# Values and transposed probabilities of a 32-row branch laid out in 128-row tiles, with zero rows below

## The chip, the cores and the metric

The kernel runs on one core of a Trainium2 chip. The metric is the device time of one execution in microseconds (us); the time before is the median of three runs. Engines are named as the profile names them: PE (TensorE, matrix products), PEld (its weight loads), DVE (VectorE), ACT (ScalarE), POOL (GpSimd), SP (SyncE, which issues the DMA transfers).

## The reference

One transformer layer on 512 tokens of width 1024, in float32: a gated feed-forward part (FFN), a mixer of two attention groups, a second FFN, a last norm. The change lies in the first attention group, which adds up three branches per token; the first of them attends to 31 compressed blocks of keys and values:

```python
def nsa_group(q, kc_raw, vc_raw, ...):
    kc = compress_blocks(kc_raw, ...)      # 31 blocks of 32 tokens, stride 16
    vc = compress_blocks(vc_raw, ...)
    ...
    s = jnp.where(mask_c, s - slopes * dist_c, NEG_INF)
    p_cmp = jnp.where(mask_c, jax.nn.softmax(s, axis=-1), 0.0)
    o_cmp = jnp.einsum('bgrtc,bcgd->btgrd', p_cmp, vc)      # contracts over the 31 blocks
    ...
    return g[..., 0:1] * o_cmp + g[..., 1:2] * o_slc + g[..., 2:3] * o_win
```

There are 8 query heads in 2 groups of 4, and the head width is 64.

## The kernel before

The kernel is one long Python program over a scheduling layer: it writes the work down in some order, and the layer fixes a list of instructions for each engine from its own estimate of costs, and the semaphore waits between them. Each engine works through its list in order. Products are made in a 32-bit format that keeps fewer bits (`F32R`), so a value is kept as two parts, high and low: ACT makes the high part by a cast, DVE the low part by a subtraction, and PE makes two or three products in place of one.

The mixer is cut into attention stages. A stage `Nsa(g, i, br)` handles group `g`, query block `i` of 128 tokens and branch `br`. `scores` makes the scores of four heads on PE (lines 838, 839, 918, 922, 923), DVE finds maxima (L911), ACT takes exponentials (L912), DVE and ACT scale them (L973 to L989). `outputs` then goes through a list `work` of blocks of keys. For each one `transposed` lets PE transpose the probabilities of four heads into one bank (L847), ACT copies the high part out (L849) and DVE the low part (L850) into a tile `u`; then `times_values` multiplies both by the values, in two products of 512 columns that add up in the bank `pv` (L884, L885). For the windows of the sequence a block has 128 keys. The compressed branch has one block of 32 rows (31 blocks and one row of zeros): its values are `CV`, a tile of 32 partitions with the two parts of both groups, its probabilities fill `u[:32]`, and its two products contract over 32 rows. It comes last in the list of the stage that closes a query block; with two groups and four query blocks that makes 8 stages and 16 such products. After the last product of a stage `put_o` takes the result out of `pv` (L855, L860, L866, L867); there is one `pv` bank.

While attention runs, pieces of other work (projections, products with the output weights, L207 to L209) are put between its steps on PE; their weights come through `split_next`, which splits a loaded tile into two parts (L97 on ACT, L98 on DVE). Units of 1024 numbers per partition come from one pool, `flat` and `unit`, with 32 buffers (`NU`); each buffer is given out again when the last reader of its tile is done.

```python
NU, NT8, NTMP, NRAW = 32, 4, 10, 4
work.append((cl, slice(0, 32), 32, CV[:, g].rearrange("p a d -> p (a d)")))
```

Of the kernel before, what the change touches and what calls it, by code (L numbers as in the profile page):

```python
# [10 lines left out]
F32R = mybir.dt.float32r  # L11
BF16 = mybir.dt.bfloat16
AF = mybir.ActivationFunctionType
ALU = mybir.AluOpType
AX = mybir.AxisListType

P = 128
# [5 lines left out]
HD = 64  # L23
# [21 lines left out]
def tile_hybrid(ctx, tc, xT, f1_wi, f1_wo, wm_t, wm_n, cw1, cw2, small, wm_oa, wm_ob, wm_oc, f2_wi, f2_wo, const, out):  # L45
    nc = tc.nc
    V, A, PE = nc.vector, nc.scalar, nc.tensor

    sb = ctx.enter_context(tc.tile_pool(name="sb", bufs=1))
    psp = ctx.enter_context(tc.tile_pool(name="psp", bufs=1, space=bass.MemoryType.PSUM))  # L50

    def f(ap):
        return ap.bitcast(F32)

    def ps(tag="mm"):
        return psp.tile([P, 512], F32, tag=tag, name=tag, bufs=NB[tag])
# [8 lines left out]
    def flat(dt=F32R):  # L65
        return sb.tile([P, 1024], dt, tag="u", name="u", bufs=NU)

    def unit(dt=F32R):
        return flat(dt).rearrange("p (a t) -> p a t", a=2)
# [4 lines left out]
    def tmp():  # L74
        return sb.tile([P, 512], F32, tag="tmp", name="tmp", bufs=NTMP)
# [6 lines left out]
    ones = sb.tile([P, P], F32, tag="ones", name="ones")  # L82
# [578 lines left out]
        yield from mm3_steps(o, wh, wl, ALLK, xs, True, True)  # L661


    CV = sb.tile([32, 2, 2, HD], F32R, tag="cv", name="cv")

    def compressed(kv):
        o = ps()
# [55 lines left out]
    def network_o(kv):  # L723
        hT, w2 = state["hT", kv]
        po = ps()
        if kv == 0:
            for c in range(2):
                PE.matmul(po[:HD, :62], w2[:, c, :], hT[:, c, :], start=c == 0, stop=c == 1)
            kc = tmp()
            V.memset(kc[:HD, :64], 0.0)  # L730
            V.tensor_copy(
                kc[:HD, :64].rearrange("p (g c) -> p g c", g=2)[:, :, :NCMP],
                po[:HD, :62].rearrange("p (g c) -> p g c", g=2),
            )
            for g in range(2):
                put_key(kc[:HD, g * 32 : g * 32 + 32], 0, KT[g][0][:, 512:544], KT[g][1][:, 512:544])
        else:
            vc = tmp()
            V.memset(vc[:32, :128], 0.0)
            for g in range(2):  # L740
                for c in range(2):
                    PE.matmul(
                        po[:NCMP, g * HD : (g + 1) * HD], hT[:, c, g * NCMP : (g + 1) * NCMP], w2[:, c, :],
                        start=c == 0, stop=c == 1,
                    )
            V.tensor_copy(vc[:NCMP, :128], po[:NCMP, :128])
            vcv = vc[:32, :128].rearrange("p (g d) -> p g d", g=2)
            A.copy(CV[:, :, 0, :], vcv)
            V.tensor_tensor(CV[:, :, 1, :], vcv, f(CV[:, :, 0, :]), op=ALU.subtract)
        yield 0.6  # L750


# [4 lines left out]
    def put_key(src, g, k1, k2):  # L757

        own = slice(g * HD, (g + 1) * HD)
        oth = slice((1 - g) * HD, (2 - g) * HD)  # L760
        A.copy(k1[own], src)
        V.tensor_tensor(k2[own], src, f(k1[own]), op=ALU.subtract)
        nc.sync.dma_start(f(k1[oth]), f(k1[own]))
        nc.sync.dma_start(f(k2[oth]), f(k2[own]))
# [79 lines left out]
    def transposed(pl, rows, cols):  # L844
        pt = ps()
        for r in range(4):
            PE.transpose(pt[:rows, r * P : (r + 1) * P], pl[r][:, cols], ident)  # L847
        u = unit()
        A.copy(u[:rows, 0, :], pt[:rows, :])  # L849
        V.tensor_tensor(u[:rows, 1, :], pt[:rows, :], f(u[:rows, 0, :]), op=ALU.subtract)  # L850
        return u
# [17 lines left out]
    def times_values(work, pv, first, last):  # L869

        ahead = None
        for n in range(len(work) + 1):
            if n < len(work):
                pl, cols, rows, v = work[n]
                cur = transposed(pl, rows, cols), rows, v
                if n == 0:
                    yield 0.44
            else:
                cur = None
            if ahead is not None:  # L880
                u, rows, v = ahead
                a = first and n == 1
                b = last and n == len(work)
                PE.matmul(pv, v, u[:rows, 0, :], start=a, stop=False)  # L884
                PE.matmul(pv, v, u[:rows, 1, :], start=False, stop=b)  # L885
                yield 0.87 if n < len(work) else 0.43
            ahead = cur

    class Nsa:
# [102 lines left out]
        def outputs(self):  # L992
            g, i, br = self.g, self.i, self.br
            if br != 2:
                state["pv"] = ps("pv")
            pv = state["pv"]

            def values_of(b, kb):
                return VT[b][:, kb, g].rearrange("p a d -> p (a d)")

            if br == 0:
                work = [(self.p, slice(b * P, (b + 1) * P), P, values_of(b, 0)) for b in range(2)]
            else:
                work = [(self.p, slice(kb * P, (kb + 1) * P), P, values_of(br - 1, kb)) for kb in range(i + 1)]
            if br != 1:
                cl = [self.c[:, r, :] for r in range(4)]
                work.append((cl, slice(0, 32), 32, CV[:, g].rearrange("p a d -> p (a d)")))
            yield from times_values(work, pv, br != 2, br != 1)
            if br != 1:
                put_o(pv, g * 2, i)  # L1010

    class Swa:
# [45 lines left out]
        def outputs(self):  # L1058
            g, i, W, c0 = self.g, self.i, self.W, self.c0
            pv = ps("pv")  # L1060
            work = [
                (self.p, slice(n * P, (n + 1) * P), P, VT[2][:, c0 // P + n, g].rearrange("p a d -> p (a d)"))
                for n in range(W // P)
            ]
            yield from times_values(work, pv, True, True)
            put_o(pv, 4 + g * 2, i)
# [84 lines left out]
    piece("c1", compressed(1))  # L1151
    piece("kw", keys(3, "w"))
    piece("o0", network_o(0))
    piece("n1", network(1))
    piece("q4", queries(4))
    piece("q5", queries(5))
    piece("o1", network_o(1))
    piece("q6", queries(6))
    piece("q7", queries(7))
# [115 lines left out]
```

## Time and profile before

| | |
|---|---|
| Time, median of 3 runs | 1015.99 us (1015.99 to 1016.55) |
| Time of the profiled execution | 1014.31 us |
| Its span, first to last instruction | 1012.5 us |
| PE busy | 982.1 us, 97% of the span |
| DVE busy | 804.2 us, 79% |
| ACT busy | 509.6 us, 50% |
| DMA, share of 16 engines | 26.8% for the loads and stores |

PE is busy nearly all the time, but products overlap in the records, so a long record is not yet time lost: what counts is the distance from the start of one product to the start of the next. The profiled execution lies 1.81 us above its own span, and 1.68 us below the median of the three runs.

### The profile page before, as it was taken

The page shows a single profiled execution, that of the slowest core. Times are in us where ns is not written, and L with a number is a line of the kernel's source. Part 1 is how long each engine was busy: PE and PEld are TensorE (multiplying, and loading weights), DVE is VectorE, ACT ScalarE, POOL GpSimd, SP SyncE. Part 2 cuts the span into 40 slices and gives each one's busy share as a digit, 9 for nine tenths or more (in the row PEclk, how much of TensorE's full clock was granted, in tenths as well). Part 3 has the DMA queues.
Part 4 walks back from the last instruction along what each step waited for, and adds up shares of the span by engine and source line. Part 5 has one row for each costly group of instructions (what it writes and reads, how often), then busy time and mean ns, then how long its engine had stood idle before and what let it go on. Part 6 is the DMA issues. An engine that isn't in the chain of part 4 may idle for free.

```text
span 1012.5 us, 15908 instructions
## 1 busy us (share of the span) xinstructions
PE 982.1 (97%) x6196; PEld 869.0 (86%) x6196; DVE 804.2 (79%) x1466; ACT 509.6 (50%) x1034; POOL 0.2 (0%) x4
## 2 busy tenths in 40 slices
PE   7799999999999999999999999989999999999997
PEld 5589999999999889788777777769999999999996
DVE  5889878788796675787889898788986878879665
ACT  7544434444344355554677675854434445344344
POOL 0000000000000000000000000000000000000000
PEclk9899999999999999999999999989999999999998
DMA  7053233222324303123311111115322323322112
GB/s 294 1 187 111 77 115 123 87 105 73 114 84 140 122 34 113 42 84 99 117 42 45 40 43 63 48 50 172 116 90 98 136 73 106 113 75 95 42 43 84
DMA packets 36508, 93.62 MB, mean 92 GB/s; under 512 B 4432, under 2 KB 8912, under 8 KB 36432
## 3 DMA queue, kind: packets, MB, share of 16 engines
q1 hardware_dynamic: 36432, 92.59, 26.8%
q8 instruction: 49, 0.80, 0.3%
q14 instruction: 27, 0.22, 0.1%
HBM read 88.87 MB, written 2.10 MB: 90 GB/s over the span
## 4 chain that ended last, share of the span: by engine, by line
PE 89%; DVE 6%; ACT 4%; issue 1%; DMA 1%; SPq 0%; DVEq 0%; ACTq 0%
PE mm L306 9%; PE mm L305 9%; PE mm L307 9%; PE sc L209 8%; PE sc L208 8%; PE sc L207 8%; PE mm L207 4%; PE mm L209 4%; PE mm L208 4%; PE sc L306 4%; PE sc L307 4%; PE sc L305 4%; PE mm L847 3%; PE pv L884 2%; PE pv L885 2%; PE mm L703 1%
## 5 line engine op out<-in xcount | busy, mean ns | idle before, releaser
L306 PE MATMUL mm<-u 128*128 128x256 f32 x760 | 214.5, 282 | 0.0
L307 PE MATMUL mm<-u 128*128 128x256 f32 x760 | 214.4, 283 | 0.0
L305 PE MATMUL mm<-u 128*128 128x256 f32 x760 | 214.3, 282 | 0.0
L207 PE MATMUL sc<-u 128*128 128x512 f32 (+1 forms) x400 | 156.5, 391 | 13.0 <-ACT u L97 12.0
L209 PE MATMUL sc<-u 128*128 128x512 f32 (+1 forms) x400 | 155.4, 388 | 0.8 <-DVE u L98 0.8
L208 PE MATMUL sc<-u 128*128 128x512 f32 (+1 forms) x400 | 155.8, 390 | 0.0
L305 PEld LDWEIGHTS mm<-u 128*128 128x128 f32 x760 | 144.5, 190 | 7.2 <-DVE tmp L512 0.5
L306 PEld LDWEIGHTS mm<-u 128*128 128x128 f32 x760 | 144.8, 191 | 5.6
L307 PEld LDWEIGHTS mm<-u 128*128 128x128 f32 x760 | 144.7, 191 | 0.6
L207 PE MATMUL mm<-u 128*128 128x512 f32 (+1 forms) x248 | 100.3, 404 | 4.6 <-ACT u L97 4.6
L209 PE MATMUL mm<-u 128*128 128x512 f32 (+1 forms) x248 | 96.6, 389 | 0.8 <-DVE u L98 0.8
L208 PE MATMUL mm<-u 128*128 128x512 f32 (+1 forms) x248 | 95.7, 386 | 0.6 <-DVE u L163 0.6
L207 PEld LDWEIGHTS sc<-u 128*128 128x128 f32 x400 | 77.3, 193 | 21.0 <-ACT u L97 12.9
L209 PEld LDWEIGHTS sc<-u 128*128 128x128 f32 x400 | 76.4, 191 | 20.4 <-DVE u L98 2.6
L307 PE MATMUL sc<-u 128*128 128x256 f32 x304 | 85.9, 283 | 0.0
L306 PE MATMUL sc<-u 128*128 128x256 f32 x304 | 85.9, 283 | 0.0
L305 PE MATMUL sc<-u 128*128 128x256 f32 x304 | 85.7, 282 | 0.0
L208 PEld LDWEIGHTS sc<-u 128*128 128x128 f32 x400 | 77.2, 193 | 6.5
L357 ACT CAST u<-tmp 128x512 fp32r<-128x512 f32 (+1 forms) x96 | 54.7, 583 | 45.4 <-PE sc L209 22.6
L380 DVE SCALAR_TENSOR_TENSOR h<-sc,h 128x512 f32<-128x512 f32 x85 | 58.3, 686 | 12.3 <-PE sc L209 12.3
L358 DVE TENSOR_TENSOR u<-tmp,u 128x512 fp32r<-128x512 f32 (+1 forms) x96 | 60.9, 640 | 8.9 <-ACT u L357 8.7
L493 ACT COPY mm<-sc 128x256 f32<-128x256 f32 x38 | 13.6, 357 | 94.7 <-PE sc L307 94.2
(221 smaller groups left out, 1994.4 us busy)
## 6 DMA issues: line engine op xcount, KB each, us to landing
t<-in_f_wi_dram SPq DMA_DIRECT2D x86, 512.0 KB, 4.4
tmp<-in_f_wo_dram SPq DMA_DIRECT2D x80, 256.0 KB, 4.7
t<-in_wm_t_dram SPq DMA_DIRECT2D x13, 512.0 KB, 4.4
t<-in_cw_dram SPq DMA_DIRECT2D x8, 512.0 KB, 4.9
tmp<-in_f_wo_dram SPq DMA_DIRECT2D x16, 128.0 KB, 4.0
t<-in_wm_oa_dram SPq DMA_DIRECT2D x4, 512.0 KB, 4.1
out_dram<-tmp SPq DMA_DIRECT2D x8, 256.0 KB, 2.1
t<-in_wm_n_dram SPq DMA_DIRECT2D x4, 408.0 KB, 3.7
```

The source lines that it names most:

```text
L207: PE.matmul(o, wh[:, c], xs[k][:, 0, :], start=s0, stop=False)
L208: PE.matmul(o, wh[:, c], xs[k][:, 1, :], start=False, stop=False)
L209: PE.matmul(o, wl[:, c], xs[k][:, 0, :], start=False, stop=s1)
L305: PE.matmul(o, w[0][:, c], x[k][0], start=new, stop=False, skip_group_check=not first)
L306: PE.matmul(o, w[0][:, c], x[k][1], start=False, stop=False, skip_group_check=not first)
L307: PE.matmul(o, w[1][:, c], x[k][0], start=False, stop=k == 3, skip_group_check=not first)
L357: A.copy(u[:, 0, :n], raw[:, :n])
L358: V.tensor_tensor(u[:, 1, :n], raw[:, :n], f(u[:, 0, :n]), op=ALU.subtract)
L380: V.scalar_tensor_tensor(h[:, i, :], o, 0.5, h[:, i, :], op0=ALU.mult, op1=ALU.add)
L847: PE.transpose(pt[:rows, r * P : (r + 1) * P], pl[r][:, cols], ident)
L884: PE.matmul(pv, v, u[:rows, 0, :], start=a, stop=False)
L885: PE.matmul(pv, v, u[:rows, 1, :], start=False, stop=b)
```

## The change

`CV` becomes a tile of 128 partitions. A unit `ct` is taken from the pool of 32 once, for the transposed probabilities of the compressed branch, in place of a new unit in each of the 8 stages. Both are filled with zeros in advance by three ACT instructions that read the constant `ones` with scale 0. Rows 0 to 31 are then written as before, in each stage, by ACT and DVE; rows 32 to 127 stay zero in both operands, and add nothing. The two products per stage run over all 128 rows. The transposes and the copies out still handle 32 rows.

```diff
-    CV = sb.tile([32, 2, 2, HD], F32R, tag="cv", name="cv")
+
+    CV = sb.tile([P, 2, 2, HD], F32R, tag="cv", name="cv")
+    ct = unit()
+    zero = ones.unsqueeze(1).to_broadcast([P, 4, P])
+    A.activation(CV.rearrange("p g a d -> p (g a d)").rearrange("p (a t) -> p a t", t=P), zero[:, :2], AF.Copy, scale=0.0)
+    for a in range(2):
+        A.activation(ct[:, a, :].rearrange("p (a t) -> p a t", t=P), zero, AF.Copy, scale=0.0)
...
-            A.copy(CV[:, :, 0, :], vcv)
-            V.tensor_tensor(CV[:, :, 1, :], vcv, f(CV[:, :, 0, :]), op=ALU.subtract)
+            A.copy(CV[:32, :, 0, :], vcv)
+            V.tensor_tensor(CV[:32, :, 1, :], vcv, f(CV[:32, :, 0, :]), op=ALU.subtract)
...
-        u = unit()
+        u = unit() if rows == P else ct
         A.copy(u[:rows, 0, :], pt[:rows, :])
         V.tensor_tensor(u[:rows, 1, :], pt[:rows, :], f(u[:rows, 0, :]), op=ALU.subtract)
...
-                PE.matmul(pv, v, u[:rows, 0, :], start=a, stop=False)
-                PE.matmul(pv, v, u[:rows, 1, :], start=False, stop=b)
+                PE.matmul(pv, v, u[:, 0, :], start=a, stop=False)
+                PE.matmul(pv, v, u[:, 1, :], start=False, stop=b)
```

From `transposed` on, lines of the changed kernel have numbers 6 higher (L884 becomes L890, L850 becomes L856). The scheduling layer also places some instructions differently. The first place is on ACT, at the passage from the first FFN to the mixer. What stands there in the changed kernel (L162 and L170 take the norm's inputs, L97 splits weights, L186 is the square root of the norm, L199 its broadcast):

```order
L162 ACTIVATE u<-h,sm 128x512
L170 ACTIVATE tmp<-h 128x512
L670 ACTIVATE u<-ones 128x512 x2
L97 CAST u<-t_3497 128x816
L186 ACT_TABLE_LOAD
L186 ACTIVATE rc<-pv,epsc 128x4
```

The two L670, which fill `ct`, are new there; all else on ACT stands as it did. The fill of `CV` stands at the very start of ACT's list, between the first table load and the copy of `epsc`. `ct` gets a buffer whose last reader is a product of the first FFN (an L307) that stands some 140 instructions ahead of the norm's products L184 on PE.

The second place is on PE, in the seventh of the 8 stages, group 1 and query block 2 (`pv<-u,cv` are the two products in question, `sc` are scores of the next stage, `mm` of L207 to L209 the output weights). Before:

```order
L209 MATMUL mm<-u 128x512
L884 MATMUL pv<-u,cv 128x512
L885 MATMUL pv<-u,cv 128x512
L838 MATMUL sc<-t_4395,u 128x32
L839 MATMUL sc<-t_4395,u 128x32
L922 LDWEIGHTS u
L922 MATMUL sc<-dch,u 128x32
L923 LDWEIGHTS u
L923 MATMUL sc<-dcl,u 128x32
L838 MATMUL sc<-t_4395,u 128x512
L839 MATMUL sc<-t_4395,u 128x512
L918 MATMUL sc<-u 128x512
```

In the changed kernel, from the row ahead of the long score product on:

```order
L929 MATMUL sc<-dcl,u 128x32
L844 MATMUL sc<-t_4399,u 128x512
L890 MATMUL pv<-u,cv 128x512
L845 MATMUL sc<-t_4399,u 128x512
L924 MATMUL sc<-u 128x512
L844 MATMUL sc<-t_4399,u 128x512
L845 MATMUL sc<-t_4399,u 128x512
L891 MATMUL pv<-u,cv 128x512
```

The pair, which stood together ahead of the next stage's scores, now stands among them, seven and eleven rows later. The third place is on DVE at the same time. Before:

```order
L850 TENSOR_TENSOR u<-mm,u 128x512 x2
L973 TENSOR_TENSOR su<-su,ge 128x4
L850 TENSOR_TENSOR u<-mm,u 32x512
L974 RECIPROCAL su<-su 128x4
L1077 TENSOR_TENSOR h<-mm,h 128x512
L985 TENSOR_SCALAR tmp<-tmp,su 128x512 x3
```

And in the changed kernel:

```order
L856 TENSOR_TENSOR u<-mm,u 128x512 x2
L98 TENSOR_TENSOR u<-t_5474,u 128x1024
L979 TENSOR_TENSOR su<-su,ge 128x4
L856 TENSOR_TENSOR u<-mm,u 32x512
L980 RECIPROCAL su<-su 128x4
L917 TENSOR_REDUCE nm<-sc 128x1
L991 TENSOR_SCALAR tmp<-tmp,su 128x512 x3
```

A split of weights (L98) has come forward, ahead of the low part of the 32 rows and of the scaling L991; on ACT its high part (L97) has come forward with it. A sum into `h` (L1077) has gone behind, and a maximum (L917) has come ahead of the scaling. In the last stage the two splits after the 32 rows have come ahead of them in the same way. All earlier lists are the same but for one product, which has moved by five rows in the fifth stage.

## Rows read from the trace of the kernel before

**Rows 1.** The page: the span, and the chain that ended last, by engine

```profile
span 1012.5 us, 15908 instructions
...
PE 89%; DVE 6%; ACT 4%; issue 1%; DMA 1%; SPq 0%; DVEq 0%; ACTq 0%
```

**Rows 2.** Source view of L884: duration ns min/median/max, first and last start, forms

```profile
L884 PE MATMUL pv<-u x54: 387/400/501, 419.2 to 621.5; 128*128 128x512 f32 x54
...
L884 PE MATMUL pv<-u,cv x8: 492/497/500, 509.4 to 622.8; 32*128 32x512 f32 x8
```

**Rows 3.** Timeline of PE, first stage: start us, duration us, engine, line, operation, shapes

```profile
508.31 0.39 PE L885 MATMUL pv<-u 128*128 128x512 f32 x1
508.54 0.39 PE L884 MATMUL pv<-u 128*128 128x512 f32 x1
508.77 0.29 PE L838 MATMUL sc<-t,u 128*128 128x288 f32 x1
...
509.03 0.40 PE L885 MATMUL pv<-u 128*128 128x512 f32 x1
509.35 0.50 PE L884 MATMUL pv<-u,cv 32*128 32x512 f32 x1
509.78 0.19 PE L922 MATMUL sc<-dch,u 128*128 128x32 bf16 x1
```

**Rows 4.** The timeline of the weight loads at the same place

```profile
508.31 0.19 PEld L884 LDWEIGHTS pv<-u 128*128 128x128 f32 x1
...
509.35 0.18 PEld L884 LDWEIGHTS pv<-u,cv 32*128 32x128 f32 x1 [0.27 <-issue]
```

**Rows 5.** Timeline of PE in the third stage, where the two stand together

```profile
542.56 0.39 PE L209 MATMUL mm<-u 128*128 128x512 f32 x1
542.88 0.49 PE L884 MATMUL pv<-u,cv 32*128 32x512 f32 x1
543.22 0.39 PE L885 MATMUL pv<-u,cv 32*128 32x512 f32 x1
543.54 0.50 PE L918 MATMUL sc<-u 128*128 128x512 f32 x1
543.87 0.40 PE L207 MATMUL mm<-u 128*128 128x512 f32 x1
```

**Rows 6.** The chain of waits, first stage: start us, us on it, what

```profile
509.42 0.43 PE pv L884
```

**Rows 7.** Windows: us, busy us of PE, PEld, DVE, ACT, POOL; granted clock

```profile
526.00:546.00 20.00, 18.56 (x98) 13.72 (x97) 19.15 (x46) 15.81 (x43) 0.00 (x0) 1.00 0.01 1
546.00:626.00 80.00, 79.44 (x453) 61.76 (x452) 69.42 (x176) 57.22 (x173) 0.00 (x0) 1.00 0.16 54
```

**Rows 8.** Waits of PE from 526 to 626 us: us in total, times, longest

```profile
PE sc L838 <- ACT tmp L912: 1.0, 2, 0.7
PE sc L838 <- ACT u L912: 0.6, 1, 0.6
```

**Rows 9.** Timeline of ACT from the first FFN to the mixer; brackets: idle before

```profile
372.06 0.61 ACT L170 ACTIVATE tmp<-h 128x512 f32<-128x512 f32 x1
372.58 0.86 ACT L97 CAST u<-t 128x816 fp32r<-128x816 f32 x1
...
376.52 0.26 ACT L186 ACTIVATE rc<-pv,epsc 128x4 f32<-128x4 f32 x1 [1.77 <-PE pv L184]
```

**Rows 10.** The timeline of ACT at the start

```profile
3.52 0.63 ACT L167 ACTIVATE acc<-h 128x512 f32<-128x512 f32 x1 [1.31 <-DMA h<-in_xT_dram]
```

**Rows 11.** The timeline of DVE in the seventh stage

```profile
603.26 0.68 DVE L850 TENSOR_TENSOR u<-mm,u 32x512 fp32r<-32x512 f32 x1 [0.29 <-ACT u L849]
...
604.64 1.27 DVE L985 TENSOR_SCALAR tmp<-tmp,su 128x512 f32<-128x512 f32 x3
...
608.40 1.22 DVE L98 TENSOR_TENSOR u<-t,u 128x1024 fp32r<-128x1024 f32 x1
```

**Rows 12.** The timeline of PE there: the transposes that read the scaled probabilities

```profile
607.06 0.60 PE L847 MATMUL mm<-ident,tmp 128*128 128x128 f32 x4
```

## The prediction

> **What bounds the kernel now.** I read the page first: the chain of waits that ended last lies on PE for 89% of the span [rows 1]. A second off PE's list is therefore likely a second off the time, where PE itself is the one that is waited for. Next the source view of L884 with its forms kept apart: 54 products over 128 rows have a median record of 400 ns, the 8 over 32 rows one of 497 ns [rows 2], though both stream 512 columns. A record overlaps its neighbours, so I went to the timeline and took distances between starts. In the first stage a product over 128 rows starts 0.23 us after the one before it, and the next one 0.23 us later (508.31, 508.54, 508.77). The 32-row product starts 0.32 us after its predecessor (509.03 to 509.35), and what follows starts 0.43 us after it (509.78) [rows 3]. The weight loads say why: the load for the 128-row L884 of 508.54 starts when the product before it does, at 508.31; the load for the 32-row product starts with that product itself, at 509.35, after 0.27 us in which the loader did nothing [rows 4]. Its 0.18 us lies open: 0.18 and 0.23 are nearly the 0.43. So in this trace a product over 32 rows lets nothing be loaded ahead of it, and its neighbours stand back as well.
>
> **What it removes.** The cost per product has three parts, each against 0.23 us. Ahead of it: 0.32 less 0.23, that is 0.09. After it: 0.43 less 0.23, 0.20. And the load of the next full product can't be made ahead either: in the third stage, where both stand together, the starts run 542.56, 542.88, 543.22, 543.54, 543.87 [rows 5], distances of 0.32, 0.34, 0.32 and 0.33, together 1.31 where four normal ones are 0.92. Such a pair costs 0.39; the last distance is the neighbour's, 0.10. Going through the other stages by the same starts, 12 of the 16 products stand alone and cost 0.29 to 0.30 each (3.55 us); after 7 of these a long product in the same format follows and costs another 0.10 (0.72); where short bf16 products or a row of transposes follow, nothing more. The two pairs (third and seventh stage) cost 0.39 and some 0.30. Together 3.55, 0.72, 0.39 and 0.30 are 4.96 us: **5.0 us**. Bounds: 6.4 if each of the 16 cost 0.40, 0 if the shape is not what makes it.
>
> What the products cost afterwards is taken from the 128-row L884 and L885 with the same 512 columns, the same tiles `pv` and `u` and the same kinds of waits [rows 3, 4].
>
> Does it reach the end? The products stand on the chain of waits, 0.43 us in the row of the first one [rows 6]; I found all 16 on it. In the first stage the chain goes on through ACT's L855, which waits for the stage's last product; it too comes earlier. From 546 to 626 us PE is busy for 79.44 of 80 us [rows 7], and over 526 to 626 us it waits 1.6 us for ACT's exponentials in its longest waits [rows 8]; these start from PE's own scores. I take the whole 5.0, with the absorbed case as a rival.
>
> A page speaks against this change. The Trainium skill, "TensorE: Matmul & The Clock Gate", section "Why this matters for your kernels", says that a single product over 32 rows takes the same time as one over 128 and that only running several at once gains. By that page the sum would be 0; [rows 3] have 0.43 us against 0.23, so here the measurement decides.
>
> **What it adds.** Three ACT fills. The two of `ct` are bounded by the neighbouring ACT instructions on 128x512, 0.61 us (L170) [rows 9], so 1.2 us together. They come after the last L170, ahead of the first cast L97, whose end moves from 373.44 to about 374.7, and the table load behind it ends near 376.0 instead of 374.75; `rc` starts at 376.52 after 1.77 us of idle time [rows 9], waiting for PE. The idle time covers the 1.2 us, by 0.5 us. Without it the norm and the first weights of the mixer would be late by up to 1.2 us. The buffer that `ct` gets is long free there. The fill of `CV`, half the size, comes at the start, where ACT sits idle for 1.31 us ahead of L167, waiting for a load [rows 10]. Cost of all three: 0, at worst 1.2 us.
>
> **What it moves.** In the seventh stage the split L98 (1.22 us) comes ahead of the 32-row low part L850 and of the scaling L985. L850 started at 603.26 and would start near 604.5, L985 at 604.64 and would start near 605.9 [rows 11]. Waiting for these are the pair's second product, which has itself gone eleven rows back, and the transposes L847, which start at 607.06 [rows 12]. The first scaled head was there some 2 us before, the third 1.15 us before (604.64 and 1.27 are 605.91). A shift of 1.2 us about uses that up. Ahead of L847 the same products stand as before, only in another order, so I count 0, with 0.3 to either side, and 1.2 us as the worst. In exchange, scores of the next stage are ready earlier. In the last stage DVE does the splits in time it spent waiting.
>
> **Sum.** The profiled execution took 1014.31 us with a span of 1012.5; less 5.0 that is 1009.3 and 1007.5. It lies 1.7 us below the median of the runs, 1015.99, so against the median I predict **1011.0 us**.
>
> **Rivals.**
> - Absorbed in part. From 526 to 546 us DVE is busy for 19.15 of 20 us and PE idles for 1.44 [rows 7]. If DVE sets the pace there, what the first three stages save (0.57, 0.69 and 0.39, 1.65 us) is waited away: 3.3 us are left, 1012.7 us. For it speaks DVE's load, against it that the chain runs on PE at these products.
> - The row count isn't the cause: the place is (the waits for fresh halves of `u`), and a 128-row product there costs the same. Then nothing is gained, 1016.0 us. That is also the time by the skill's page above. Against it: 128-row L884 wait in the same way and start 0.23 us apart [rows 3].
> - Slower: `ct` holds one of the 32 buffers of `u` through the mixer. If a split of weights has to wait for a buffer and PE for the split, each case costs about 0.86 us for the cast and 1.22 for the subtraction [rows 9, 11], 2.1 us. From the third case on the saving is gone; four give 1016.0 less 5.0 plus 8.4, 1019.4 us. Against it: each stage took a buffer for these 32 rows anyway, and in the built program the splits wait for nearly the same instructions as before.
> - More than counted: all 16 cost 0.40, 1009.6 us.
>
> **How the numbers follow.** Forecast 0.72 (1009.9 to 1012.2 in itself), absorbed 0.13, no effect 0.07, slower by buffers 0.05, more 0.03. The range runs from 1009.5, just under the largest saving, to 1013.6, where half of the saving is lost, and leaves out the cases of no effect and of buffers and the tails, under 2 in 10. 0.2% of the time, about what a measurement of this kernel can tell from no change, is 2.0 us, so faster means below 1014.0. Forecast, absorbed and more end there, less 0.02 for an absorbed case that ends above it: faster 0.86; same 0.09; slower 0.05.
>
> **What would show it.** Right: the products `pv<-u,cv` over 128 rows have records near 400 ns and start 0.23 us after the one before, their weight load starts with that one, and PE's rows from the first such product to the last (509.35 to 623.70 now) take about 4.5 us less; the stretch from 372 to 377 us is unchanged. Wrong: starts still 0.3 to 0.4 us apart at these places (the row count isn't it), the same stretch no shorter though the starts are closer, with longer idle times of PE before L838 or L847 (absorbed), PE waiting for L97 or L98 inside the mixer (buffers), or `rc` of the second norm on ACT after 377 us (the fills).

## The result and the profile after

The changed kernel takes **1010.31 us** in the median of six runs (1009.76 to 1012.77), against 1015.99 (1015.09 to 1017.62) for the kernel before in the same group of runs: a ratio of 0.9949, 95% interval 0.9935 to 0.9963, or 5.7 us less. A later group of runs gave 1011.39 against 1016.06, ratio 0.9948 (0.9935 to 0.9960), 4.7 us less. The forecast was 1011.0 us, with a range from 1009.5 to 1013.6.

The profiled execution took 1010.24 us. The page has the span, PE's busy time and the chain, to be held against [rows 1]:

```profile
span 1008.5 us, 15912 instructions
...
PE 977.1 (97%) x6196; PEld 868.9 (86%) x6196; DVE 803.8 (80%) x1466; ACT 511.3 (51%) x1037; POOL 0.2 (0%) x4
...
PE 89%; DVE 5%; ACT 4%; issue 1%; DMA 1%; SPq 0%; DVEq 0%; ACTq 0%
```

The bound is the same, PE. The source view of L890, which was L884, shows the products in their new form beside the 54 that were over 128 rows already (duration ns min/median/max, first and last start):

```profile
L890 PE MATMUL pv<-u x54: 387/407/505, 420.6 to 618.7; 128*128 128x512 f32 x54
...
L890 PE MATMUL pv<-u,cv x8: 388/394/397, 510.7 to 619.9; 128*128 128x512 f32 x8
```

Their median fell from 497 ns [rows 2] to 394. The distances count more. PE's timeline in the first stage, in answer to [rows 3]:

```profile
510.46 0.40 PE L891 MATMUL pv<-u 128*128 128x512 f32 x1
510.69 0.39 PE L890 MATMUL pv<-u,cv 128*128 128x512 f32 x1
510.92 0.19 PE L928 MATMUL sc<-dch,u 128*128 128x32 bf16 x1
```

The distances are 0.23 and 0.23, where they were 0.32 and 0.43. The timeline of the weight loads there, in answer to [rows 4]: the load for the product of 510.69 begins at 510.46, with the product before it.

```profile
510.46 0.19 PEld L890 LDWEIGHTS pv<-u,cv 128*128 128x128 f32 x1
```

In the third stage, where the two products stand together, all distances are now 0.23 or 0.24, where [rows 5] have 0.32 to 0.34:

```profile
542.84 0.40 PE L209 MATMUL mm<-u 128*128 128x512 f32 x1
543.07 0.39 PE L890 MATMUL pv<-u,cv 128*128 128x512 f32 x1
543.31 0.39 PE L891 MATMUL pv<-u,cv 128*128 128x512 f32 x1
543.54 0.40 PE L924 MATMUL sc<-u 128*128 128x512 f32 x1
543.77 0.39 PE L207 MATMUL mm<-u 128*128 128x512 f32 x1
```

ACT's timeline at the passage from the first FFN to the mixer, in answer to [rows 9], has the two new fills (L670) between the last L170 and the first cast L97:

```profile
373.54 0.61 ACT L170 ACTIVATE tmp<-h 128x512 f32<-128x512 f32 x1
374.06 1.14 ACT L670 ACTIVATE u<-ones 128x512 fp32r<-128x512 f32 x2
375.11 0.86 ACT L97 CAST u<-t 128x816 fp32r<-128x816 f32 x1
375.99 1.28 ACT L186 ACT_TABLE_LOAD   x1
378.00 0.26 ACT L186 ACTIVATE rc<-pv,epsc 128x4 f32<-128x4 f32 x1 [0.73 <-PE pv L184]
```

The idle time ahead of `rc` fell from 1.77 to 0.73 us, by 1.04: the fills stand in time that ACT spent waiting for PE, and `rc` is still released by PE. From L170 to `rc` it is 4.46 us, as before (378.00 less 373.54, and 376.52 less 372.06).

**A yardstick free of the rest.** L186 is the root of a norm, and there is one at each end of the mixer. From the first to the second the kernel before takes 649.58 less 376.52, 273.06 us, and the changed kernel 646.03 less 378.00, 268.03 us. The two rows on ACT's timeline, of before and of after (the first ones are in [rows 9] and above):

```profile
649.58 0.26 ACT L186 ACTIVATE rc<-pv,epsc 128x4 f32<-128x4 f32 x1
```

```profile
646.03 0.26 ACT L186 ACTIVATE rc<-pv,epsc 128x4 f32<-128x4 f32 x1
```

That is **5.03 us** less, within the mixer alone. In what follows "root to root" is this stretch; where two numbers stand behind it in brackets, they are the starts of the two roots. It repeats well: 273.03 in a second profile of the kernel before, 267.91 in one of the changed kernel. The stretches outside it vary by themselves: from the second root to the end of the span the changed kernel took 362.47 us in one profile and 363.49 in the other.

### The profile page after: what moved, and what is told of

Read it like the earlier page. It is cut to its first block, busy times and chain, and to the rows that moved or that the text cites. A ratio compares the mean times of both kernels' runs of the same rounds, so it can differ in the third digit from the quotient of the medians.

```text
span 1008.5 us, 15912 instructions
## 1 busy us (share of the span) xinstructions
PE 977.1 (97%) x6196; PEld 868.9 (86%) x6196; DVE 803.8 (80%) x1466; ACT 511.3 (51%) x1037; POOL 0.2 (0%) x4
## 4 chain that ended last, share of the span: by engine, by line
PE 89%; DVE 5%; ACT 4%; issue 1%; DMA 1%; SPq 0%; DVEq 0%; ACTq 0%
PE mm L306 9%; PE mm L307 9%; PE mm L305 9%; PE sc L209 8%; PE sc L208 8%; PE sc L207 8%; PE mm L207 4%; PE mm L209 4%; PE mm L208 4%; PE sc L306 4%; PE sc L307 4%; PE sc L305 4%; PE mm L853 2%; PE pv L890 2%; PE pv L891 1%; PE mm L709 1%
## 5 line engine op out<-in xcount | busy, mean ns | idle before, releaser
L307 PE MATMUL mm<-u 128*128 128x256 f32 x760 | 214.4, 283 | 0.0
L207 PE MATMUL sc<-u 128*128 128x512 f32 (+1 forms) x400 | 156.4, 391 | 13.5 <-ACT u L97 12.0
L209 PE MATMUL sc<-u 128*128 128x512 f32 (+1 forms) x400 | 155.2, 388 | 1.4 <-DVE u L98 1.4
L307 PEld LDWEIGHTS mm<-u 128*128 128x128 f32 x760 | 144.6, 190 | 0.6
L207 PE MATMUL mm<-u 128*128 128x512 f32 (+1 forms) x248 | 100.1, 404 | 4.6 <-ACT u L97 4.6
L209 PE MATMUL mm<-u 128*128 128x512 f32 (+1 forms) x248 | 96.8, 390 | 0.8 <-DVE u L98 0.8
L207 PEld LDWEIGHTS sc<-u 128*128 128x128 f32 x400 | 77.2, 193 | 21.9 <-ACT u L97 13.3
L209 PEld LDWEIGHTS sc<-u 128*128 128x128 f32 x400 | 76.3, 191 | 20.7 <-DVE u L98 2.9
L307 PE MATMUL sc<-u 128*128 128x256 f32 x304 | 85.9, 283 | 0.0
```

The lines of the kernel that those rows point to most:

```text
L207: PE.matmul(o, wh[:, c], xs[k][:, 0, :], start=s0, stop=False)
L209: PE.matmul(o, wl[:, c], xs[k][:, 0, :], start=False, stop=s1)
L307: PE.matmul(o, w[1][:, c], x[k][0], start=False, stop=k == 3, skip_group_check=not first)
```

## The experiments

**Rows alone, everything else as changed.** Four kernels keep the changed kernel's tiles, fills, lists and shared unit, and differ only in the number of rows that the products use. The first goes back to 32 rows:

```diff
-                PE.matmul(pv, v, u[:, 0, :], start=a, stop=False)
-                PE.matmul(pv, v, u[:, 1, :], start=False, stop=b)
+                k = P if rows == P else 32
+                PE.matmul(pv, v[:k], u[:k, 0, :], start=a, stop=False)
+                PE.matmul(pv, v[:k], u[:k, 1, :], start=False, stop=b)
```

> Everything of the changed kernel (tiles of 128 rows, fills, the shared unit, the same lists on every engine), but the 16 products contract over rows 0 to 31 alone, as before. Row count is the cause: starts 0.32 us after the predecessor and 0.42 to 0.43 us to the next come back; from the first rc (L186) of the mixer to that of the second FFN about 273.0 us (273.1 before, 268.0 after), time 1015.5 to 1016.5. Rival, that the fills, the lists or the shared unit made it faster: about 268 us and 1010.3.

Measured: 1016.01 us against 1016.06 for the kernel before, ratio 1.0002 (0.9994 to 1.0011); root to root 273.26 (377.60, 650.86). In the first stage the starts are 0.33 us apart ahead of the 32-row product and 0.43 behind it (510.14, 510.47, 510.90). The whole gain is gone with the row count, and the fills, the moved L97 and L98 and the shared unit together cost or gain nothing that shows.

The second uses 64 rows (`k = ... else 64`), the third 96. These two and the fourth ran once each, so they are read from root to root.

> As the changed kernel with the same lists, the 16 products over rows 0 to 63. If anything short of the full array loses the early weight load: distances as with 32 rows, 273 us from rc to rc. If the loss grows with the missing rows: two thirds of it, 271.4 us. If only 32 rows are special: 268 us.

> As the changed kernel with the same lists, the 16 products over rows 0 to 95. If anything short of 128 rows loses the early load: 273 us from rc to rc. If the loss grows with the missing rows: a third of it, 269.7 us. If only products that fit in half of the array lose it: 268 us.

Measured: with 64 rows 1015.98 us, root to root 273.09 (378.02, 651.11); with 96 rows 1011.93 us and 268.02 (378.61, 646.63). PE's timeline in the first stage, for 64 rows and then for 96:

```profile
510.43 0.40 PE L892 MATMUL pv<-u 128*128 128x512 f32 x1
510.75 0.50 PE L891 MATMUL pv<-u,cv 64*128 64x512 f32 x1
511.19 0.19 PE L929 MATMUL sc<-dch,u 128*128 128x32 bf16 x1
```

```profile
511.01 0.40 PE L892 MATMUL pv<-u 128*128 128x512 f32 x1
511.24 0.40 PE L891 MATMUL pv<-u,cv 96*128 96x512 f32 x1
511.48 0.19 PE L929 MATMUL sc<-dch,u 128*128 128x32 bf16 x1
```

64 rows have 0.32 and 0.44, as 32 rows had; 96 rows have 0.23 and 0.24, as 128. The cost is a step between 64 and 96 rows, not a slope: over the four counts tried it does not grow with the number of rows left out.

The fourth makes only the first product of each pair 128 rows long, and the second 32.

```diff
-                PE.matmul(pv, v, u[:, 1, :], start=False, stop=b)
+                PE.matmul(pv, v[:rows], u[:rows, 1, :], start=False, stop=b)
```

> As the changed kernel with the same lists, the first product of each pair over 128 rows, the second over 32. If the costs add up product by product: eight are left at 0.29 to 0.40 us each, 2.3 to 3.2 us over the changed kernel, 270.3 to 271.2 us from rc to rc. If what costs is going from one form to another and back, once per stage: little less than with both, 272 us or more where the two stand apart.

Measured: 1013.66 us; root to root 270.73 (378.57, 649.30), 2.70 above the changed kernel. Half of the products give half of the cost, 0.34 each. The second arm of that expectation was set up wrongly: all but one of the 8 pairs stand apart here, so a cost per change is halved by this edit too. So far a cost per product and a cost per change between the two forms explain all of it. The weight loads of the kernel before, at its pair in the third stage (the same place as [rows 5]), speak for the second:

```profile
542.88 0.18 PEld L884 LDWEIGHTS pv<-u,cv 32*128 32x128 f32 x1 [0.35 <-issue]
542.98 0.18 PEld L885 LDWEIGHTS pv<-u,cv 32*128 32x128 f32 x1
543.54 0.19 PEld L918 LDWEIGHTS sc<-u 128*128 128x128 f32 x1 [0.37 <-issue]
543.64 0.19 PEld L207 LDWEIGHTS mm<-u 128*128 128x128 f32 x1
```

The load for the second 32-row product begins at 542.98, though its product starts at 543.22: it is made ahead, right behind another 32-row product. What is not made ahead is the first load over 32 rows and the first over 128 behind them.

**Pairs side by side.** The low part's product is issued first, over 32 rows. With that the scheduling layer puts the two products of a stage side by side in all 8 stages; in the first experiment they were apart in 7. The edit, against the first experiment:

```diff
+                hi, lo_ = (0, 1) if rows == P else (1, 0)
-                PE.matmul(pv, v[:k], u[:k, 0, :], start=a, stop=False)
-                PE.matmul(pv, v[:k], u[:k, 1, :], start=False, stop=b)
+                PE.matmul(pv, v[:k], u[:k, hi, :], start=a, stop=False)
+                PE.matmul(pv, v[:k], u[:k, lo_, :], start=False, stop=b)
```

> The products of the compressed branch run over 32 rows again, in tiles that are filled as in the change, and the low part's product is issued first; by that PE's list has the two products of a stage side by side in all 8 stages, where the run with 32 rows in the change's own order had them apart in 7. Theory A (PE pays for each change from products over the full array to products over half of its rows or fewer, and back): 8 such changes instead of 15, each 0.34 to 0.36 us; the stretch between the roots of the two norms on ACT is about 268.0 + 2.8 = 270.8 us, and the time about 1013.3. Theory B (each 32-row product pays by itself, since nothing is loaded ahead of it): 16 products as before, about 273.2 us and 1016.0.

Its control is the same order over 128 rows:

> The change with only the low part's product issued first: the control for the order of the paired run. Both theories: all products over 128 rows, so the order is worth nothing by itself: between the norms' roots 268.0 us, with 0.5 to either side for the moved rows; time about 1010.3.

Measured: paired over 32 rows 1012.78 us, ratio 0.9966 (0.9954 to 0.9978), root to root 270.29 (377.07, 647.36); the control 1011.26 us and 267.93 (377.17, 645.10). The two have the same lists on every engine. So 16 products over 32 rows, side by side in twos, cost 2.36 us, less than half of what 16 mostly lone ones cost. Theory B is out; A's 2.8 was somewhat too high: each trip from 128-row products to 32-row ones and back cost 0.30 in place of 0.34 to 0.36. Some of the cost is won back where PE waits in any case: ahead of a score product of the second stage it waits 0.67 us for ACT's exponentials in the paired kernel and 0.83 us in the control.

**Six in a row.** Four more 32-row products, with weights of zero (`CZ`, a tile of 32 partitions filled once by ACT), follow each pair of the paired kernel:

```diff
+    CZ = sb.tile([32, P], F32R, tag="cvz", name="cvz")
...
+    A.activation(CZ, zero[:32, 0], AF.Copy, scale=0.0)
...
-                PE.matmul(pv, v[:k], u[:k, lo_, :], start=False, stop=b)
+                PE.matmul(pv, v[:k], u[:k, lo_, :], start=False, stop=b and k == P)
+                if k < P:
+                    for x in range(4):
+                        PE.matmul(pv, CZ, u[:k, lo_, :], start=False, stop=b and x == 3)
```

> The paired kernel over 32 rows, with four more products over 32 rows right behind each pair; their weights are a tile of zeros, so they add nothing to the output. Theory A (the cost lies in the change of form and the product behind it): the starts inside the six go 0.32 to 0.34 us apart at the first and 0.23 us apart from the second or third on; the four add 0.93 us per stage, 7.4 in all. Theory B (products over 32 rows are slower one by one): all of them 0.32 to 0.34 us apart, 1.3 us per stage and 10.6 in all. By A the stretch between the norms' roots is about 277.7 us, by B 280.9, with 1 us to either side since the order of other rows changes.

Measured, in one run: root to root 278.04 us (377.06, 655.10; A: 277.7, B: 280.9), time 1020.39. PE's timeline in the third stage; the row with x4 is four products, its start that of the first:

```profile
543.68 0.39 PE L209 MATMUL mm<-u 128*128 128x512 f32 x1
544.00 0.49 PE L894 MATMUL pv<-u,cv 32*128 32x512 f32 x1
544.34 0.39 PE L895 MATMUL pv<-u,cv 32*128 32x512 f32 x1
544.57 1.09 PE L898 MATMUL pv<-u,cvz 32*128 32x512 f32 x4
545.59 0.51 PE L931 MATMUL sc<-u 128*128 128x512 f32 x1
545.93 0.40 PE L207 MATMUL mm<-u 128*128 128x512 f32 x1
546.17 0.40 PE L208 MATMUL mm<-u 128*128 128x512 f32 x1
```

The first distance is 0.32, the second 0.34, the third 0.23. The four take 1.02, which is three of 0.23 and one of 0.33; then come 0.34 and 0.24. So 32-row products follow each other as fast as 128-row ones. Each change of form costs some 0.10 at the change and 0.11 at the next distance, in either direction, about 0.4 for going and coming back when long products stand on both sides. With a lone 32-row product the distance after going is also the one of coming back: that is the 0.43 of [rows 3], 0.20 above 0.23.

**The changed kernel again, and one product in place of two.** With a tile of 128 rows there is room for both parts at once: the low part goes to rows 32 to 63 of the high part's tile, the values stand there once more, and one product over 128 rows adds up both. The second fill of `ct` falls away.

```diff
-    for a in range(2):
-        A.activation(ct[:, a, :].rearrange("p (a t) -> p a t", t=P), zero, AF.Copy, scale=0.0)
+    A.activation(ct[:, 0, :].rearrange("p (a t) -> p a t", t=P), zero, AF.Copy, scale=0.0)
...
+            A.copy(CV[32:64, :, 0, :], vcv)
+            V.tensor_tensor(CV[32:64, :, 1, :], vcv, f(CV[:32, :, 0, :]), op=ALU.subtract)
...
-        V.tensor_tensor(u[:rows, 1, :], pt[:rows, :], f(u[:rows, 0, :]), op=ALU.subtract)
+        low = u[:, 1, :] if rows == P else u[32:64, 0, :]
+        V.tensor_tensor(low, pt[:rows, :], f(u[:rows, 0, :]), op=ALU.subtract)
...
-                PE.matmul(pv, v, u[:, 0, :], start=a, stop=False)
-                PE.matmul(pv, v, u[:, 1, :], start=False, stop=b)
+                one = rows < P
+                PE.matmul(pv, v, u[:, 0, :], start=a, stop=one and b)
+                if not one:
+                    PE.matmul(pv, v, u[:, 1, :], start=False, stop=b)
```

> The changed kernel itself, on the chip of this group of runs, for comparison with the stacked version: about 1010.3 us and 268.0 us between the norms' roots under both theories.

> A version that should go further: the low part of the 32 rows is written to rows 32 to 63 of the high part's tile, the values are repeated in rows 32 to 63, and one product over 128 rows takes the place of two. Theory A: a 128-row product costs 0.23 us here, 8 fewer make 1.84: between the norms' roots about 266.2 us, time about 1008.5. Theory B gives the same. The rival here: the one product has to wait for DVE's low part, which the first of two did not, and PE idles at those places; then up to all of it is waited away, about 268.0 us and 1010.3.

Measured, on the same chip: stacked 1011.33 us (ratio to the kernel before 0.9947, 0.9933 to 0.9961), the changed kernel again 1011.39 (0.9948, 0.9935 to 0.9960). No difference can be told in the time. Root to root the stacked kernel takes 267.12 (378.21, 645.33) and the changed one 267.91 (378.70, 646.61): 0.79 us of the 1.84 arrived. That is not the price of the products alone, since the scheduling layer also ordered much of PE's and DVE's work in the mixer in another way. PE's timeline of the stacked kernel shows a wait in the first stage:

```profile
511.28 0.49 PE L893 MATMUL pv<-u,cv 128*128 128x512 f32 x1
512.15 0.41 PE L854 MATMUL mm<-ident,tmp 128*128 128x128 f32 x2 [0.38 <-DVE tmp L995]
```

Behind the one product PE idles for 0.38 us, until DVE has scaled the probabilities for the transposes. These start 133.94 us after the first root (512.15 less 378.21), in the changed kernel 133.53 (512.23 less 378.70): 0.41 later in place of 0.23 earlier. DVE's scaling itself starts 0.40 later, 133.45 us after the root (511.66 less 378.21) in place of 133.05 (511.75 less 378.70):

```profile
511.66 0.87 DVE L995 TENSOR_SCALAR tmp<-tmp,su 128x256 f32<-128x256 f32 x3
```

```profile
511.75 0.86 DVE L991 TENSOR_SCALAR tmp<-tmp,su 128x256 f32<-128x256 f32 x3
```

So this stage gained nothing because PE had to wait for a later DVE. 0.28 us of that lateness is there already at the low part of the 32 rows (510.54 less 378.21 is 132.33, 510.75 less 378.70 is 132.05), ahead of the product that was saved. How the 1.05 us that are missing spread over the stages was not traced.

**The kernel before, profiled again.**

> The kernel before, profiled a second time. In the profile shown of it, the root of the mixer's norm on ACT starts at 376.52 us, in all nine profiles of kernels with the fills between 377.07 and 378.70. If the fills make the first FFN longer: about 376.5 again, and a time near 1014.3. If that profile was a quick execution and the first FFN's length varies by itself: a start between 377 and 379 us, and a time near 1016. From there to the second norm's root 273.1 us under both.

Measured, in one run: 1014.73 us; the first root at 376.93, root to root 273.03 (376.93, 649.96). The start lies between the two expectations. The ten profiles with fills have it from 377.06 to 378.70. What differs lies ahead of the fills of `ct`: from the start of ACT's last L170 to `rc` all twelve profiles have 4.46 us. The norm ahead of the first FFN has a root too; it starts at 28.28 and 28.51 us without fills, and with them between 28.49 and 29.55. From there to the mixer's root it is 348.24 and 348.42 us without, and from 348.31 to 349.15 with them. In both stretches the two groups overlap, so fills need not lengthen either; that the one of `CV` costs nothing at all is not shown by so few profiles. The timed runs leave little room: with 32 rows and all fills the time stood at 1.0002 of before (at most 1.1 us by its interval), and the gains of the changed kernel in two groups (5.7 and 4.7) and of its control (4.8) are 5.1 us on average, what root to root alone gives.

## Why the prediction came out right, and where its reasons fell short

- **The sum.** 4.96 us were summed, and root to root measured 5.03 (5.12 between the second profiles, 273.03 less 267.91). That it fits to 0.07 us is in part luck: with the lists of the changed kernel, where the pair of the seventh stage stands apart, the same products cost 5.23 (273.26 less 268.03). Distances between starts were the right thing to read; the difference of the records' lengths, 0.10 us for 16 products, would have given 1.6.
- **The step that was told wrongly** is "in this trace a product over 32 rows lets nothing be loaded ahead of it". It is right for the first of them and for the first 128-row product behind them. Inside the pair of [rows 5] the second 32-row load was made ahead, and six in a row showed 32-row products 0.23 us apart. The cost belongs to the change from products over 96 or 128 rows to products over 32 or 64, and to the change back. The sum was untouched by that since 12 products stood alone, each with a change before and behind it, and the two pairs had been read off as they stood. Counted in trips there and back, the cost is nearly the same in four kernels; counted in products it is not:

| Kernel | 32-row products | Trips | Cost against 128 rows, us | Per trip | Per product |
|---|---|---|---|---|---|
| Before | 16 | 14 | 5.03 | 0.36 | 0.31 |
| First experiment, mostly apart | 16 | 15 | 5.23 | 0.35 | 0.33 |
| Fourth, second product alone | 8 | 8 | 2.70 | 0.34 | 0.34 |
| Paired | 16 | 8 | 2.36 | 0.30 | 0.15 |

In the kernel before, 6 of the 14 trips have short products or transposes right behind; that is in part why they come to less than the 0.4 with long products on both sides.

- **The rule that spoke against the change.** The rows decided rightly. The sentence of the Trainium skill, "TensorE: Matmul & The Clock Gate", section "Why this matters for your kernels", that a single product over 32 rows takes as long as one over 128 holds between 32-row products (0.23 us apart, six in a row) but not at the change. Another page has what fits: the Trainium skill, "TensorEngine Tiling (Array Packing)", section "Key Properties", says that changing the tiling mode drains the engine, while changing only the tile does not. The trace agrees as far as it goes: 0.32 to 0.34 us in place of 0.23 at each change, and none with 96 rows, a count that is not among those which the Trainium skill lists on that page, in the section "Available Configurations" (32, 64 and 128 rows). That the engine is drained no run here shows.
- **The fills** cost nothing that shows, as forecast: two took 1.14 us together (1.2 was the bound), the idle time ahead of `rc` fell by 1.04, and what ends it is still PE. The sign that was named for them, `rc` after 377 us, did come (378.00), but the delay arose ahead of them: from L170 on nothing is later. The one of `CV` stands at the start of ACT's list ahead of L167, which starts at 3.50 us (3.52 in [rows 10]).
- **The moved split in the seventh stage** was set at 0. DVE's scalings L985 start 228.12 us after the first root before (604.64 less 376.52), and as L991 225.62 us after it now (603.62 less 378.00), 2.50 us earlier though L98 stands ahead of them. The forecast had L98 push them near 605.9 in the times of before, with the savings of the stages ahead not yet taken off; these are larger than the 1.22 us of L98. PE waits for L991 in none of its longer waits (for L985 before, 0.2 us, once).
- **The absorbed case** did not come. The windows of [rows 7] now read

```profile
526.00:546.00 20.00, 18.58 (x101) 14.31 (x100) 18.85 (x44) 16.17 (x43) 0.00 (x0) 1.00 0.01 1
546.00:626.00 80.00, 79.50 (x468) 64.94 (x467) 72.61 (x182) 57.75 (x173) 0.00 (x0) 1.00 0.18 60
```

PE idles no more than before, and its longest waits over 526 to 626 us are to the digit those of [rows 8], so DVE and ACT kept up:

```profile
PE sc L844 <- ACT tmp L918: 1.0, 2, 0.7
PE sc L844 <- ACT u L918: 0.6, 1, 0.6
```

Something like the absorbed case showed in the stacked version: there PE waited for a later DVE in the first stage, and that stage gained nothing.

- **Buffers.** Between the two roots PE waits for L98 for 0.2 us, once (0.3 us, once, before), and not for L97 in any of its longer waits; with 32 rows over the same shared unit the time was that of before.
- **The stretch from the first of these products to the last** was to take about 4.5 us less. It takes 3.48 less, 110.87 us (510.69 to 621.56) against 114.35 (509.35 to 623.70). The forecast overlooked that in the last stage the second product has moved back, from two rows behind the first to seven. With these lists and 32 rows (first experiment) the stretch is 115.64 us (510.47 to 626.11), so the row count is worth 4.77 in it.
- **What the profiles add on their own.** The span fell by 4.0 us, not 5.03: the first root came 1.48 later, and the rest after the second root took some 0.45 us less. In the second pair of profiles the first root came 1.77 later, and the rest took some 0.45 more (363.49 against 363.04). These stretches differ between executions of one kernel by up to 1 us, so a difference of this size in one pair of profiles can't be put down to the change.

## What to carry to other kernels

Read what a small product costs from the distances of its neighbours' starts and from where the weight loads begin, not from its record. Where products over 64 or 32 rows stand singly among products over the full array, filling them up with zero rows to 96 or 128 (once, in a tile that stays), gave back 0.30 to 0.36 us here for each trip saved, and putting them side by side 0.42 (7 trips, 273.26 less 270.29 us), at 512 columns and with PE as the engine that is waited for. A further product saved may bring less, if the work behind it waits for another engine, as in the stacked version's first stage.

## What was not expected of the hardware

- 64 rows cost what 32 do (root to root 273.09 and 273.26 us), 96 what 128 do (268.02 and 268.03).
- 32-row products in a row start 0.23 us apart, like full ones. The price stands at the change, about 0.1 us there and 0.11 at the next distance, and it is the same in both directions.
